# A transformer layer on one core: the later rows of the ada weight are asked for from GpSimd's queue instead of the sync engine's

## The chip, the cores and the metric

The kernel runs on one core of a Trainium2 chip. Its time is the device time of one execution in microseconds (us); of several executions the median is given. A core has a matrix engine (PE), a vector engine (DVE), an activation engine (ACT), GpSimd (POOL) and a sync engine (SP). Each runs its own instructions in order and waits on semaphores. Transfers between the chip's memory and the on-chip buffer are asked for by an instruction in some engine's queue, here SP's or POOL's, and are then moved by 16 DMA engines that all queues share.

## What is computed

One layer for 256 tokens of width 2048, in float32. A conditioning vector gives nine modulation vectors of 2048 each, and these shift, scale and gate three sub-layers:

```python
ada = (jax.nn.silu(c) @ w_ada + b_ada)[:, None, :]          # w_ada: 2048 x 18432
sh1, sc1, g1, sh2, sc2, g2, sh3, sc3, g3 = jnp.split(ada, N_ADA, axis=-1)
h = _swiglu(_modulate(x, sh1, sc1), ffn1_w_in, ffn1_w_out)
x = _layernorm(ALPHA * x + 0.5 * (1 + g1) * h, ln1_g, ln1_b)
h = _token_mixer(_modulate(x, sh2, sc2), w_in, ...)         # attention and mLSTM heads
x = _layernorm(ALPHA * x + (1 + g2) * h, ln2_g, ln2_b)
h = _swiglu(_modulate(x, sh3, sc3), ffn2_w_in, ffn2_w_out)
x = _layernorm(ALPHA * x + 0.5 * (1 + g3) * h, ln3_g, ln3_b)
```

All weights are read once from memory. The product with `w_ada` has one row on the left, so it needs 151 MB of weights and hardly any arithmetic.

## The kernel before

**The big products.** Each weight matrix comes in pieces of 1 MB, `raw` tiles, of which three buffers exist. `load_w` (L379) asks for a piece on SP (L383 or L387), ACT casts it to a rounded `hi` part (L155), DVE subtracts to get the remainder `lo` (L156), and PE multiplies hi by hi, hi by lo and lo by hi (L420 to L422, or L425 and L426). There are six `hi` and six `lo` buffers of half a piece each. A `raw` buffer is free for SP's next request when DVE's last subtraction of it has ended.

**The ada product** is spread over the whole run beneath the big products. It has 18 units of 16 rows; a row is 128 x 1024 numbers, 0.5 MB. For every row a DMA fills a tile `ar`, and DVE multiplies it by a column of silu(c) and adds it to an accumulator (`ada_acc`, L168 for the first row, L170 for the others). The accumulator is `acc`, or a part of the tile `gate`. When the 16 rows of a unit are in, its tail splits the accumulator into hi and lo (`alo`, L156), sums it over the partitions with PE (`bc`, L183) and stores columns (`pair_tail`) or a gate row (`gate_tail`). `gate_tail` also asks POOL for a piece of `b_ada` (L212), which may land only after the split has read the accumulator beneath it.

**Which rows are asked for where.** The first unit is loaded at the start on SP (`first_ada0`, L905). The next three units (`first_ada`, L937) have three `ar` buffers and are asked for from POOL, but for three rows. The remaining 14 units, 224 rows, go through the class `AdaQueue`: `pump(n)` is called after each weight piece with a rate (1 to 1.42 rows) and traces that many rows through `ada_rows` (L186 to L191), whose DMA at L189 has two `ar` buffers. These are the later rows. Row k + 2 can be asked for only when DVE has added row k.

**The order of the work.** The program is traced in Python, and a scheduler in the tile framework orders each engine's queue by its own estimates of when an instruction's inputs are ready; at the boundaries between the sub-layers the DVE order is written by hand. PE's order is that of the code. `pinned` (L141) and `issue_after` add ordering edges on DVE and ACT.

**POOL's other work:** a few memsets, the `pow` that gives reciprocal roots (L287: `rs`, `mr` at the three boundaries, `rr` in the mixer), the `b_ada` pieces at L212 and the layer-norm parameters `lg`, `lb` at L595 and L596.

**Stages by time:** the start and the first columns of FFN 1 to 226 us, the rest of its first product to about 520, its second product to 750, a boundary to about 790, the mixer to 1150, a boundary, FFN 2 from about 1180 to the end. The last row is asked for at 1518 us.

Of the kernel before, what the change touches and what calls it, by code (L numbers as in the profile page):

```python
# [14 lines left out]
P = 128  # L15
# [17 lines left out]
def layer_kernel(  # L33
# [8 lines left out]
    V, S, G_, PE, SP = nc.vector, nc.scalar, nc.gpsimd, nc.tensor, nc.sync  # L42
# [123 lines left out]
    def ada_acc(acc, raw, k):  # L166
        if k == 0:
            V.tensor_scalar_mul(acc, raw, csil[:, k:k + 1])  # L168
        else:
            V.scalar_tensor_tensor(out=acc, in0=raw, scalar=csil[:, k:k + 1], in1=acc,  # L170
                                   op0=ALU.mult, op1=ALU.add)
# [14 lines left out]
    def ada_rows(acc, src, tag):  # L186
        for k in range(KD):
            raw = ap.tile(list(acc.shape), F32, tag="araw", bufs=2, name=f"ar{tag}_{k}")
            SP.dma_start(raw, src[k * P:(k + 1) * P])  # L189
            ada_acc(acc, raw, k)  # L190
            yield  # L191

# [26 lines left out]
    class AdaQueue:  # L219
# [4 lines left out]
        def pair(self, v, j, where=None, stage=0):  # L224
            self.units.append((where, stage, lambda acc: ada_rows(acc, pair_cols(v, j), f"{v}_{j}"),
                               lambda acc: pair_tail(acc, v, j), [P, 2, 512], f"{v}_{j}"))

        def gate(self, v, s, *where, stage=0):
            for j in range(2):
                cols = w_ada[0, :, v * D + j * 1024:v * D + (j + 1) * 1024]  # L230
                self.units.append((where[j], stage, lambda acc, cols=cols, j=j: ada_rows(acc, cols, f"{v}_{j}"),
                                   lambda acc, j=j: gate_tail(acc, v, j, s), [P, 1024], f"{v}_{j}"))
# [1485 lines left out]
```

## Time and profile before

| | |
|---|---|
| median of 3 runs | 1874.08 us (1870.46 to 1882.13) |
| the profiled execution | 1878.46 us, span of its instructions 1876.8 us |
| PE busy | 1829.0 us, 97% of the span |
| DVE busy | 1465.0 us, 78% |
| ACT busy | 911.8 us, 49% |
| POOL busy | 62.2 us, 3% |
| moved by DMA | 510.74 MB, mean 272 GB/s |
| `ar` rows asked for from SP, from POOL | 230, 45 |

The times differ from run to run by some tenths of a per cent. A busy PE is not always PE at its peak, so what PE waits for is read from the list of waits. In a row of that list, or of a group of instructions, the name behind the arrow is that of the work that ended the wait. SP and POOL instructions that ask for a transfer appear under the line that asks, and the time to landing is counted from the start of the request to the semaphore of the transfer.

### The profile page before, as it was taken

The page shows a single profiled execution, that of the slowest core. Times are in us where ns is not written, and L with a number is a line of the kernel's source. Part 1 is how long each engine was busy: PE and PEld are TensorE (multiplying, and loading weights), DVE is VectorE, ACT ScalarE, POOL GpSimd, SP SyncE. Part 2 cuts the span into 40 slices and gives each one's busy share as a digit, 9 for nine tenths or more (in the row PEclk, how much of TensorE's full clock was granted, in tenths as well). Part 3 has the DMA queues.
Part 4 walks back from the last instruction along what each step waited for, and adds up shares of the span by engine and source line. Part 5 has one row for each costly group of instructions (what it writes and reads, how often), then busy time and mean ns, then how long its engine had stood idle before and what let it go on. Part 6 is the DMA issues. An engine that isn't in the chain of part 4 may idle for free.

```text
span 1876.8 us, 29775 instructions
## 1 busy us (share of the span) xinstructions
PE 1829.0 (97%) x11881; PEld 1673.8 (89%) x11881; DVE 1465.0 (78%) x1883; ACT 911.8 (49%) x1320; POOL 62.2 (3%) x92
## 2 busy tenths in 40 slices
PE   7999999999999999999989999999999999999997
PEld 5999999999998888699989887888999999988887
DVE  6888989778788886878879788988977766574655
ACT  3554363443454433845556545565444454554441
POOL 1211200000000000100000000000000000000000
PEclk9999999999999999999999999999999999999999
DMA  9988978999998898489978894998878776666664
GB/s 365 383 279 294 333 232 274 313 312 325 296 315 305 309 329 296 136 301 331 316 254 307 303 314 142 307 305 265 271 253 265 260 241 193 201 202 204 205 204 146
DMA packets 283906, 510.74 MB, mean 272 GB/s; under 512 B 10834, under 2 KB 134386, under 8 KB 282744
## 3 DMA queue, kind: packets, MB, share of 16 engines
q1 hardware_dynamic: 275656, 477.90, 75.0%
q0 software_dynamic: 8112, 30.95, 4.8%
q8 instruction: 93, 1.52, 0.3%
q14 instruction: 45, 0.37, 0.1%
HBM read 506.71 MB, written 2.10 MB: 271 GB/s over the span
## 4 chain that ended last, share of the span: by engine, by line
PE 38%; DMA 10%; DVE 8%; issue 2%; ACT 2%; POOL 0%; DVEq 0%; ACTq 0%; SPq 0%; POOLq 0%
PE gu_f L425 9%; DMA ar<-in_w_ada_dram 7%; PE gu_f L426 4%; PE o_f L421 4%; PE o_f L420 4%; PE o_f L422 4%; PE fs L425 3%; DMA raw_fh<-in_ffn_w_in_dram 2%; DVE acc L170 2%; PE fs L426 1%; DVE gate L170 1%; PE fh L425 1%; PE b_mv L421 1%; PE b_mv L420 1%; PE b_mv L422 1%
## 5 line engine op out<-in xcount | busy, mean ns | idle before, releaser
L170 DVE SCALAR_TENSOR_TENSOR acc<-ar,csil,acc 128x1024 f32<-128x1024 f32 (+1 forms) x167 | 211.7, 1269 | 74.3 <-DMA ar<-in_w_ada_dram 73.7
L425 PE MATMUL gu_f<-x_f,hi_f2i 128*128 128x512 f32 x768 | 251.8, 382 | 0.0
L422 PE MATMUL s<-x_f,lo_s 128*128 128x256 f32 x768 | 211.9, 276 | 0.8 <-DVE lo_s L156 0.7
L420 PE MATMUL s<-x_f,hi_s 128*128 128x256 f32 x768 | 212.2, 277 | 0.2 <-ACT x_f L336 0.2
L421 PE MATMUL s<-x_f,hi_s 128*128 128x256 f32 x768 | 212.0, 276 | 0.0
L426 PE MATMUL gu_f<-x_f,lo_f2i 128*128 128x256 f32 x768 | 209.3, 273 | 0.0
L422 PE MATMUL gu_f<-x_f,lo_f1i 128*128 128x256 f32 x640 | 176.4, 276 | 1.4 <-DVE lo_f1i L156 1.3
L421 PE MATMUL gu_f<-x_f,hi_f1i 128*128 128x256 f32 x640 | 176.0, 275 | 0.0
L420 PE MATMUL gu_f<-x_f,hi_f1i 128*128 128x256 f32 x640 | 176.0, 275 | 0.0
L156 DVE TENSOR_TENSOR lo_f2o<-raw_f2o,hi_f2o 128x1024 fp32r<-128x1024 f32 x86 | 105.2, 1225 | 86.9 <-ACT hi_f2o L155 86.8
L156 DVE TENSOR_TENSOR lo_f2i<-raw_f2i,hi_f2i 128x1024 fp32r<-128x1024 f32 x96 | 117.5, 1224 | 65.7 <-ACT hi_f2i L155 64.8
L425 PEld LDWEIGHTS gu_f<-x_f,hi_f2i 128*128 128x128 f32 x768 | 145.1, 189 | 20.3
L155 ACT CAST hi_s<-raw_s 128x1024 fp32r<-128x1024 f32 x96 | 99.5, 1051 | 128.7 <-PE s L421 77.0
L422 PEld LDWEIGHTS s<-x_f,lo_s 128*128 128x128 f32 x768 | 147.9, 193 | 1.2 <-DVE lo_s L156 1.2
L421 PEld LDWEIGHTS s<-x_f,hi_s 128*128 128x128 f32 x768 | 147.9, 193 | 0.4 <-DVE x_f L339 0.4
L420 PEld LDWEIGHTS s<-x_f,hi_s 128*128 128x128 f32 x768 | 147.8, 193 | 0.3 <-ACT x_f L336 0.3
L426 PEld LDWEIGHTS gu_f<-x_f,lo_f2i 128*128 128x128 f32 x768 | 147.4, 192 | 0.2
L155 ACT CAST hi_f2o<-raw_f2o 128x1024 fp32r<-128x1024 f32 x86 | 90.0, 1047 | 115.7 <-PE o_f L422 107.5
L155 ACT CAST hi_f2i<-raw_f2i 128x1024 fp32r<-128x1024 f32 x96 | 100.4, 1045 | 91.3 <-PE gu_f L425 65.3
L155 ACT CAST hi_f1o<-raw_f1o 128x1024 fp32r<-128x1024 f32 x86 | 88.5, 1047 | 113.7 <-DMA raw_f1o<-in_ffn_w_out_dram 55.0
L170 DVE SCALAR_TENSOR_TENSOR gate<-ar,csil,gate 128x1024 f32<-128x1024 f32 (+1 forms) x94 | 117.6, 1252 | 29.0 <-DMA ar<-in_w_ada_dram 28.9
L155 ACT CAST hi_f1i<-raw_f1i 128x1024 fp32r<-128x1024 f32 x80 | 81.3, 1049 | 111.6 <-DMA raw_f1i<-in_ffn_w_in_dram 80.2
(449 smaller groups left out, 5095.4 us busy)
## 6 DMA issues: line engine op xcount, KB each, us to landing
ar<-in_w_ada_dram SPq DMA_DIRECT2D x230, 512.0 KB, 5.5
raw_f2i<-in_ffn_w_in_dram SPq DMA_DIRECT2D x48, 1024.0 KB, 5.2
raw_s<-in_ffn_w_in_dram SPq DMA_DIRECT2D x47, 1024.0 KB, 7.6
raw_f1o<-in_ffn_w_out_dram SPq DMA_DIRECT2D x44, 1024.0 KB, 7.3
raw_f2o<-in_ffn_w_out_dram SPq DMA_DIRECT2D x44, 1024.0 KB, 5.2
raw_f1i<-in_ffn_w_in_dram SPq DMA_DIRECT2D x40, 1024.0 KB, 7.8
ar<-in_w_ada_dram POOLq DMA_DIRECT2D x45, 512.0 KB, 6.4
raw_mxo<-in_w_out_dram SPq DMA_DIRECT2D x16, 1024.0 KB, 7.7
```

The source lines that it names most:

```text
L155: S.copy(hi, src)
L156: return V.tensor_tensor(out=lo, in0=src, in1=hi.bitcast(F32), op=ALU.subtract)
L170: V.scalar_tensor_tensor(out=acc, in0=raw, scalar=csil[:, k:k + 1], in1=acc, op0=ALU.mult, op1=ALU.add)
L420: PE.matmul(o, ah, bh, start=start, stop=False)
L421: PE.matmul(o, ah, bl, start=False, stop=False)
L422: PE.matmul(o, al, bh, start=False, stop=stop)
L425: PE.matmul(o, ah, x.rearrange("p s (a n) -> p s n a", a=2), start=start, stop=False)
L426: PE.matmul(o[:, T:], al, woven(x[:, 0]), start=False, stop=stop)
```

## The change

One word in `ada_rows`: the DMA of the 224 later rows is traced on GpSimd instead of the sync engine.

```diff
     def ada_rows(acc, src, tag):
         for k in range(KD):
             raw = ap.tile(list(acc.shape), F32, tag="araw", bufs=2, name=f"ar{tag}_{k}")
-            SP.dma_start(raw, src[k * P:(k + 1) * P])
+            G_.dma_start(raw, src[k * P:(k + 1) * P])
             ada_acc(acc, raw, k)
             yield
```

Since the scheduler estimates other arrival times for the rows, it also places some instructions of DVE and ACT differently. PE's order is unchanged.

SP's queue in the mixer (about 910 to 940 us), the difference from before to after: `raw_fb` are weight pieces of the attention heads' queries, `ar_0_2` to `ar_0_5` rows of the unit that makes the first half of gate 2.

```order
 L383 DMA raw_fb_9975<-in_w_in_dram 128x4x512
 L383 DMA raw_fb_10054<-in_w_in_dram 128x4x512
-L189 DMA ar_0_2_9962<-in_w_ada_dram 128x1024
-L189 DMA ar_0_3_10043<-in_w_ada_dram 128x1024
 L383 DMA raw_fb_10126<-in_w_in_dram 128x4x512
-L189 DMA ar_0_4_10112<-in_w_ada_dram 128x1024
-L189 DMA ar_0_5_10115<-in_w_ada_dram 128x1024
 L383 DMA raw_fb_10218<-in_w_in_dram 128x4x512
```

The rows no longer stand between the weight pieces.

DVE's queue at the same place: L156 makes the `lo` parts of those weight pieces, L170 adds the rows to their accumulator.

```order
 L156 TENSOR_TENSOR lo_fb_9978<-raw_fb_9975,hi_fb_9977 128x1024
+L170 SCALAR_TENSOR_TENSOR acc_0_9893<-ar_0_2_9962,csil,acc_0_9893 128x1024
 L156 TENSOR_TENSOR lo_fb_10006<-raw_fb_9975,hi_fb_10005 128x1024
-L170 SCALAR_TENSOR_TENSOR acc_0_9893<-ar_0_2_9962,csil,acc_0_9893 128x1024
+L170 SCALAR_TENSOR_TENSOR acc_0_9893<-ar_0_3_10043,csil,acc_0_9893 128x1024
 L156 TENSOR_TENSOR lo_fb_10057<-raw_fb_10054,hi_fb_10056 128x1024
-L170 SCALAR_TENSOR_TENSOR acc_0_9893<-ar_0_3_10043,csil,acc_0_9893 128x1024
 L156 TENSOR_TENSOR lo_fb_10085<-raw_fb_10054,hi_fb_10084 128x1024
+L170 SCALAR_TENSOR_TENSOR acc_0_9893<-ar_0_4_10112,csil,acc_0_9893 128x1024
+L170 SCALAR_TENSOR_TENSOR acc_0_9893<-ar_0_5_10115,csil,acc_0_9893 128x1024
 L156 TENSOR_TENSOR lo_fb_10129<-raw_fb_10126,hi_fb_10128 128x1024
```

Each of these rows is added one `lo` earlier than before; the same happens at many places of the first 1250 us.

POOL's queue about 1000 us, where it has other work: `rr` is the `pow` for the mLSTM heads' normalization, the rows are those of the second half of gate 2.

```order
+L189 DMA ar_1_3_11004<-in_w_ada_dram 128x1024
+L189 DMA ar_1_4_11080<-in_w_ada_dram 128x1024
 L287 TENSOR_TENSOR rr<-ss,mhalf 128x8
-L212 DMA gate<-in_b_ada_dram 128x512 x2
+L189 DMA ar_1_5_11155<-in_w_ada_dram 128x1024
+L189 DMA ar_1_6_11158<-in_w_ada_dram 128x1024
```

The `pow` now stands behind row 4 of its unit and ahead of row 5, and the two `b_ada` pieces that followed it come later among the rows.

## The prediction

> **What bounds the kernel now.** I read the page first, then the list of who waits for whom, for PE, for SP's queue and, stage by stage, for DVE; then the timeline of single rows.
>
> ```profile
> span 1876.8 us, 29775 instructions
> PE 1829.0 (97%) x11881; PEld 1673.8 (89%) x11881; DVE 1465.0 (78%) x1883; ACT 911.8 (49%) x1320; POOL 62.2 (3%) x92
> ...
> ar<-in_w_ada_dram SPq DMA_DIRECT2D x230, 512.0 KB, 5.5
> ...
> ar<-in_w_ada_dram POOLq DMA_DIRECT2D x45, 512.0 KB, 6.4
> ```
>
> PE is busy for 97% of the span, so nothing that happens to the rows can be worth more than what PE waits for while the moved rows run. That is the list of PE's waits between 226 and 1518 us, the time from the first moved request to the last:
>
> ```profile
> PE sps L1428 <- DVE dm L1434: 5.0, 1, 5.0
> PE o_mx L422 <- DVE ylo L156: 2.9, 1, 2.9
> PE fh L425 <- DVE hT L1642: 2.8, 1, 2.8
> ...
> PE bc L183 <- DVE alo L156: 2.0, 2, 1.6
> PE pr_fb L422 <- DVE lo_fb L156: 1.5, 1, 1.5
> PE gu_f L422 <- DVE lo_f1i L156: 1.3, 2, 1.1
> ...
> PE b_fv L421 <- DVE lo_fv L156: 1.0, 1, 1.0
> PE b_mv L421 <- DVE lo_mv L156: 0.8, 1, 0.8
> ```
>
> Each ends with DVE (columns: total us, times, longest). Together they are 5.0 + 2.9 + 2.8 + 2.0 + 1.5 + 1.3 + 1.0 + 0.8 = 17.3 us, 0.9% of the time. This is the ceiling of a gain. For a loss there is no such ceiling: DVE works in order, and where it stands at a row that has not landed, the `lo` parts that PE needs stand behind it. DVE's waits by stage (330 to 480, 480 to 750, 790 to 950, 950 to 1130, 1180 to 1320 us), in that order:
>
> ```profile
> DVE acc L170 <- DMA ar<-in_w_ada_dram: 14.5, 7, 3.9
> DVE lo_f1i L156 <- ACT hi_f1i L155: 10.8, 5, 4.0
> DVE gate L170 <- DMA ar<-in_w_ada_dram: 10.7, 6, 4.9
> DVE acc L168 <- DMA ar<-in_w_ada_dram: 3.1, 1, 3.1
> ...
> DVE acc L170 <- DMA ar<-in_w_ada_dram: 21.0, 18, 2.5
> DVE lo_f1o L156 <- ACT hi_f1o L155: 10.9, 11, 3.0
> DVE o_f L538 <- PE o_f L422: 5.7, 1, 5.7
> ...
> DVE acc L170 <- DMA ar<-in_w_ada_dram: 13.9, 11, 3.0
> DVE gate L170 <- DMA ar<-in_w_ada_dram: 2.1, 3, 1.1
> DVE lo_mv L156 <- ACT hi_mv L155: 1.6, 2, 1.2
> DVE gate L168 <- DMA ar<-in_w_ada_dram: 1.4, 1, 1.4
> ...
> DVE acc L170 <- DMA ar<-in_w_ada_dram: 15.5, 9, 4.7
> DVE gate L170 <- DMA ar<-in_w_ada_dram: 9.1, 6, 3.7
> DVE dm L1433 <- ACT dm L1432: 4.3, 2, 2.6
> DVE acc L168 <- DMA ar<-in_w_ada_dram: 2.0, 1, 2.0
> ...
> DVE gate L170 <- DMA ar<-in_w_ada_dram: 3.5, 3, 2.9
> ```
>
> So DVE waits for rows 14, 18, 15, 16 and 3 times in these stages. In the first two it also waits 10.8 and 10.9 us for ACT's casts, so there it has room; in the mixer (790 to 1130) the rows are nearly all that it waits for, and it has little.
>
> **The change part by part.** *The request.* Does a row on SP stand behind the weight pieces? Here are a DVE addition and SP's next row, and a DVE addition and POOL's next row in the stage whose rows POOL asks for already:
>
> ```profile
> 842.95 1.29 DVE L170 SCALAR_TENSOR_TENSOR acc<-ar,csil,acc 128x1024 f32<-128x1024 f32 x1
> ...
> 844.27 0.37 SPq L189 DMA_DIRECT2D ar<-in_w_ada_dram  x1
> ...
> 117.50 1.28 DVE L170 SCALAR_TENSOR_TENSOR gate<-ar,csil,gate 128x1024 f32<-128x1024 f32 x1
> ...
> 119.09 0.72 POOL L937 DMA_DIRECT2D ar<-in_w_ada_dram  x1 [2.87 <-DVE gate L170]
> ```
>
> SP asks 0.03 us after the addition that frees the buffer (842.95 + 1.29 = 844.24), so it stands at the row before the buffer is free: the row is not late, what waits is the weight piece behind it. POOL asks 0.31 us after (117.50 + 1.28 = 118.78). The moved row is therefore asked for 0.28 us later, not sooner.
>
> *The landing.* The page's medians are 6.4 us from POOL and 5.5 from SP, 0.9 more. But the median of all rows flatters SP for those rows that DVE waits for: they are slow ones, behind weight pieces in the same queue. On the chain of waits:
>
> ```profile
> 935.93 5.10 SPq L383 DMA_DIRECT2D raw_fbk<-in_w_in_dram  x2
> 943.43 0.34 SPq L189 DMA_DIRECT2D ar<-in_w_ada_dram  x1
> ...
> 943.43 8.65 DMA ar<-in_w_ada_dram
> ```
>
> A row asked for behind two pieces took 8.65 us. In a queue of its own it would not stand behind them, so the excess of the rows that matter lies between nothing and 0.9 us. I take half, 0.45, since rows of both kinds are waited for. With the 0.28 us a round trip gets 0.73 us longer; the ends are 0.28 and 1.18. An end below zero is a rival of its own.
>
> The Trainium skill, "DMA: Bandwidth & Descriptors", section "Latency and other measured facts", speaks against the change: it gives about 1 us to the first byte for a transfer from GpSimd and about 0.6 us for one from the sync engine. By it the landing would cost an estimated 0.4 us more, the round trip 0.68 us, and the sum below would hardly differ; the trace's medians agree in sign and are further apart (0.9 us).
>
> *What DVE pays.* With two buffers, the time for which DVE stands at one row is time that the next one, already on its way, gains; so one row of two pays: waits x 0.73 / 2. By stage: 14 gives 5.1 us, 18 gives 6.6, 15 gives 5.5, 16 gives 5.8, 3 gives 1.1; 24.1 us of DVE in all.
>
> *What PE pays.* 330 to 480: DVE's room (10.8 us) covers 5.1, but PE stood at `lo_f1i` for 1.3 us already, so the lead is short at times: 1 us (0 to 5.1). 480 to 750: none of the PE waits above is from this stage, and 10.9 + 5.7 us of room cover 6.6: 0. 790 to 950: room is 1.6 us in the rows above; PE already feels `lo_fv`, `lo_mv` and `lo_fb`, 3.3 us of 17.4 that DVE waits for rows there. Between that share (1.0) and all that is left (3.9) I take 3. 950 to 1130: room 4.3 us, but PE's waits of 5.0 and 2.9 lie here: 3 (0 to 5.8). 1180 to 1320: 1 us. Sum +8.
>
> *The weight pieces on SP* lose what stood ahead of them.
>
> ```profile
> SPq L189 <- DVE acc L170: 190.8, 120, 4.2
> ...
> SPq L189 <- DVE gate L170: 112.2, 63, 5.3
> ...
> L155 ACT CAST hi_fh<-raw_fh 128x1024 fp32r<-128x1024 f32 x32 | 32.9, 1050 | 29.8 <-DMA raw_fh<-in_ffn_w_in_dram 26.8 <-PE fh L426 1.8 <-PE fh L425 1.2
> ```
>
> SP stood at rows for 190.8 + 112.2 = 303 us. That costs nothing where the `raw` buffers are full anyway. At `raw_fh`, after the second boundary, it does: ACT waits 26.8 us for these pieces and PE 2.8 us at `fh`. Earlier requests give back at most those 2.8 us and what else is lost to raw pieces, unseen; I take -3.
>
> *DVE's order.* Rows stand one `lo` earlier, so a `lo` can come one addition (1.28 us) later. At the four places where PE already stands at a `lo` (`pr_fb`, `gu_f`, `b_fv`, `b_mv`) that is 0 to 5.1 us; I take 1.
>
> *POOL.* 224 requests of 0.72 us are 161 us of an engine that is 3% busy. Ahead of them in the queue stand the L212 requests, which wait for `alo`; in DVE's order `alo` precedes the addition that frees the next row's buffer, so nothing is held. Behind a row stand the `pow` instructions: a request just begun can delay `rr` by up to 0.31 + 0.72 = 1.0 us; at the boundaries no row is due. `lg` waits long for PE, with no row behind it that is due. I take 0.
>
> Sum: 8 - 3 + 1 = +6 us. The profiled execution took 1878.46 us, 1.7 more than its span and 4.4 more than the median of the three runs; +6 makes 1884.5 for it, and 1880 as a median.
>
> **The rivals.** *Rows arrive sooner.* In a queue of their own they share the DMA engines with the weight pieces instead of following them. Then DVE's row waits shrink, and PE gets back some or all of 17.3 us: 1857 to 1869, the middle 1863. For it: the 8.65 us row. Against it: POOL's rows run beside SP's weight pieces in the stage before 226 us, and their median is 6.4.
>
> The Trainium skill, "DMA: Bandwidth & Descriptors", section "Queues, rings and completion order", has the rule that would do this: each DMA engine takes turns between queues that have work. No run here shows it by itself.
>
> *Nothing to measure.* The lead of the `lo` parts covers everything: 1874, from 1870 to 1876. For it: 480 to 750, where 21.0 us of row waits reach PE nowhere.
>
> *DVE becomes the bound in the mixer*, the rival on the other side. If its lead over PE is used up, every longer round trip passes through: at 1.18 us, 14, 15, 16 and 3 waits give 48 x 1.18 / 2 = 28 us, so 1902; at half that, 1888. It decides once DVE's added 5.5 us in 790 to 950 exceeds its room there. For it: PE waits for `lo` parts already; against it: DVE's lead is restored at the boundaries.
>
> **How the numbers follow.** Forecast (1876 to 1888): 0.45; nothing: 0.22; sooner: 0.13; the mixer bound: 0.20. Likeliest is 1880. The range, 1862 to 1900, leaves out the last part of each tail and takes in the run-to-run spread of some 4 us. About 1% (1855 to 1893) is what a measurement of this kernel can tell from no change: faster takes more than the whole ceiling, 0.05; slower is most of the mixer rival, 0.17; within it 0.78.
>
> **What would show it.** The rows under L189 on POOL, asked for 0.3 us after DVE's addition, landing at 6 to 6.4 us; DVE's waits for rows up from 17.4 and 26.6 us in the mixer; PE's waits at `lo_fv`, `lo_mv`, `lo_fb` longer, at `fh` shorter. Rows landing under 5.5 us would make the forecast wrong towards faster, PE waits of 10 us or more at mixer `lo` parts towards slower, and so would a POOL wait that holds a row.

## The result: 2.5% slower, outside the range

The changed kernel takes 1923.03 us (median of 4, 1916.45 to 1928.78), the kernel before, run beside it, 1874.03 us. The ratio is 1.0254, with a 95% interval from 1.0206 to 1.0303: 49 us lost, where the prediction had 6 and a range up to 1900. The profiled execution after took 1920.51 us. Medians leave out two far slower executions, one of 2365.48 us in run e4 and one of 4934.1 us of the kernel before beside it.

From the page of the kernel after: span, busy time, and the rows of two kinds of transfers (number, size, median us from request to landing).

```profile
span 1918.8 us, 29789 instructions
...
PE 1842.2 (96%) x11881; PEld 1680.0 (88%) x11881; DVE 1465.9 (76%) x1883; ACT 912.6 (48%) x1320; POOL 205.0 (11%) x316
...
ar<-in_w_ada_dram POOLq DMA_DIRECT2D x269, 512.0 KB, 5.4
...
raw_f1o<-in_ffn_w_out_dram SPq DMA_DIRECT2D x44, 1024.0 KB, 7.4
```

DVE's busy time is what it was (1465.0 before). PE's own busy time grew by 13.2 us with the same 11881 instructions, so 29 of the 42 us that the span grew are waits of PE, and 13 are PE being slower. The median landing of a row, 5.4 us, is no worse than SP's 5.5 before. By the signs named in the prediction a landing under 5.5 us would have meant a faster kernel, so that sign misled: one median over the whole run does not show the later landing by stage that the table below has. The other sign came true, PE waits of 10 us or more at mixer `lo` parts: `lo_m`, `lo_fb` and `lo_fv` make 10.9 us in the list below.

Where it was lost, by the first matmul of each stage: the start and the first product of FFN 1 end at the same time (526.6 us before, 526.8 after); the second product with its boundary, to the first `mo` matmul (the first product of the mixer), takes 256.1 us instead of 233.0; the mixer with its boundary, to the first `ge` (the first of FFN 2), 419.0 instead of 400.0. FFN 2 gives nothing. So 23 us went in the second product, where the prediction had 0, and 19 in the mixer.

PE's waits after, 226 to 1518 us:

```profile
PE bc L183 <- ACT ahi L155: 7.4, 1, 7.4
PE o_f L421 <- DVE lo_f1o L156: 6.0, 4, 2.3
PE pr_m L422 <- DVE lo_m L156: 4.5, 3, 2.7
PE ptp L1308 <- DVE s L1293: 4.2, 1, 4.2
PE pr_fb L422 <- DVE lo_fb L156: 3.4, 2, 2.4
PE gu_f L422 <- DVE lo_f1i L156: 3.1, 1, 3.1
PE b_fv L421 <- DVE lo_fv L156: 3.0, 2, 2.3
```

New are the waits for `lo_f1o`, and one of 7.4 us for `ahi`, the hi part of the accumulator, at the end of the second product, where before PE waited for nothing. ACT's timeline shows what held `ahi` (start, length, instruction, idle time before it): it stands behind casts of the last weight pieces, and these waited 8.18 and 0.70 us for the pieces to land.

```profile
753.74 1.99 ACT L155 CAST hi_f1o<-raw_f1o 128x1024 fp32r<-128x1024 f32 x2 [8.18 <-DMA raw_f1o<-in_ffn_w_out_dram]
756.43 1.99 ACT L155 CAST hi_f1o<-raw_f1o 128x1024 fp32r<-128x1024 f32 x2 [0.70 <-DMA raw_f1o<-in_ffn_w_out_dram]
758.33 0.61 ACT L155 CAST ahi<-acc 128x512 fp32r<-128x512 f32 x1
```

Behind both stands DVE, whose subtractions free the buffers of the pieces. Its row waits in the five stretches of the prediction, in that order (the same clock times, so after 750 us slightly earlier work):

```profile
DVE acc L170 <- DMA ar<-in_w_ada_dram: 16.3, 8, 4.0
DVE gate L170 <- DMA ar<-in_w_ada_dram: 13.1, 8, 3.6
...
DVE acc L170 <- DMA ar<-in_w_ada_dram: 41.1, 24, 3.8
...
DVE lo_f1o L156 <- ACT hi_f1o L155: 6.0, 6, 3.0
...
DVE acc L170 <- DMA ar<-in_w_ada_dram: 16.2, 10, 3.6
DVE gate L170 <- DMA ar<-in_w_ada_dram: 13.0, 8, 3.0
...
DVE gate L168 <- DMA ar<-in_w_ada_dram: 1.8, 1, 1.8
...
DVE acc L170 <- DMA ar<-in_w_ada_dram: 13.4, 6, 5.4
DVE gate L170 <- DMA ar<-in_w_ada_dram: 11.1, 7, 4.1
...
DVE gate L170 <- DMA ar<-in_w_ada_dram: 8.4, 5, 3.5
```

From 480 to 750 us they doubled, from 21.0 to 41.1 us, and from 790 to 950 they went from 17.4 to 31.0. Summed over the additions of all 224 later rows, DVE now stands 155.0 us, against 100.6 before.

How this gets through to PE is seen in what ACT waits for from 480 to 750 us; first after, then before:

```profile
ACT hi_f1o L155 <- DMA raw_f1o<-in_ffn_w_out_dram: 66.8, 20, 7.8
ACT hi_f1o L155 <- PE o_f L422: 27.4, 17, 3.4
```

```profile
ACT hi_f1o L155 <- DMA raw_f1o<-in_ffn_w_out_dram: 55.0, 21, 5.0
ACT hi_f1o L155 <- PE o_f L422: 45.2, 29, 3.5
```

Where ACT waits for PE, the casts are ahead and PE sets the pace. That fell from 45.2 to 27.4 us, and the waits for a weight piece grew from 55.0 to 66.8 us: a piece can be asked for only after DVE's last subtraction of an older one.

### The profile page after: what moved, and what is told of

Its sections match the earlier page's. It is cut to its first block, busy times and chain, and to the rows that moved or that the text cites. A ratio compares the mean times of both kernels' runs of the same rounds, so it can differ in the third digit from the quotient of the medians.

```text
span 1918.8 us, 29789 instructions
## 1 busy us (share of the span) xinstructions
PE 1842.2 (96%) x11881; PEld 1680.0 (88%) x11881; DVE 1465.9 (76%) x1883; ACT 912.6 (48%) x1320; POOL 205.0 (11%) x316
## 4 chain that ended last, share of the span: by engine, by line
PE 36%; DMA 10%; DVE 7%; issue 4%; ACT 2%; POOL 1%; DVEq 0%; POOLq 0%; ACTq 0%; SPq 0%
DMA ar<-in_w_ada_dram 9%; PE gu_f L425 9%; PE gu_f L426 4%; PE o_f L420 4%; PE o_f L421 4%; PE o_f L422 4%; PE fs L425 3%; PE fs L426 1%; PE fh L425 1%; PE o_mx L420 1%; DVE gate L170 1%; PE o_mx L421 1%; PE o_mx L422 1%; DMA raw_fh<-in_ffn_w_in_dram 1%; DVE acc L170 1%
## 5 line engine op out<-in xcount | busy, mean ns | idle before, releaser
L170 DVE SCALAR_TENSOR_TENSOR acc<-ar,csil,acc 128x1024 f32<-128x1024 f32 (+1 forms) x167 | 211.6, 1268 | 107.3 <-DMA ar<-in_w_ada_dram 106.9
L189 POOL DMA_DIRECT2D ar<-in_w_ada_dram x224 | 143.4, 640 | 999.3 <-DVE acc L170 437.5
L156 DVE TENSOR_TENSOR lo_f2o<-raw_f2o,hi_f2o 128x1024 fp32r<-128x1024 f32 x86 | 105.2, 1224 | 86.8 <-ACT hi_f2o L155 86.7
L156 DVE TENSOR_TENSOR lo_f2i<-raw_f2i,hi_f2i 128x1024 fp32r<-128x1024 f32 x96 | 117.4, 1223 | 65.6 <-ACT hi_f2i L155 64.8
L425 PEld LDWEIGHTS gu_f<-x_f,hi_f2i 128*128 128x128 f32 x768 | 145.1, 189 | 20.4
L170 DVE SCALAR_TENSOR_TENSOR gate<-ar,csil,gate 128x1024 f32<-128x1024 f32 (+1 forms) x94 | 117.5, 1251 | 48.0 <-DMA ar<-in_w_ada_dram 47.9
```

The source lines that it names most:

```text
L156: return V.tensor_tensor(out=lo, in0=src, in1=hi.bitcast(F32), op=ALU.subtract)
L189: G_.dma_start(raw, src[k * P:(k + 1) * P])
L425: PE.matmul(o, ah, x.rearrange("p s (a n) -> p s n a", a=2), start=start, stop=False)
```

## The experiments

The change does two things at once: it moves the requests to another queue, and, through the scheduler's estimates, it moves instructions on DVE and ACT. To part them, kernels were built in which the order on named engines is held to a written list, by ordering edges alone; engines that are not named keep the scheduler's order. e11 below, held in this way on DVE, ACT and SP, takes as long as the kernel before (1.0002), so the holding itself costs nothing that shows.

All numbers in one place. *Asked* is the mean time from the end of the DVE work that frees a buffer to the request of the next transfer into it, *landed* from the request to the last of the 16 closing packets of that transfer in the DMA records (the semaphore reports it some 0.45 us later); both for the second product. Their sum is the trip of a buffer, from free to full. In e4 the 4-byte transfers look like closing packets, so its landings cannot be told apart. "DVE at rows" is its row wait from 480 to 750 us. Stages, waits and trips are read from one profiled execution of each kernel; four of those that take as long as before or less (before, e4, e6, e11) agree within 0.3 us for the second product and differ by up to 7.5 us for the mixer.

| kernel | ratio to before (95%) | second product, mixer, us | DVE at rows, us | rows: asked + landed, us | pieces: asked + landed, us |
|---|---|---|---|---|---|
| before | 1 | 233.0, 400.0 | 21.0 | 0.07 + 5.22 | 0.42 + 6.55 |
| after | 1.0254 (1.0206 to 1.0303) | 256.1, 419.0 | 41.1 | 0.34 + 5.42 | 0.03 + 6.97 |
| e1, rows on POOL, old order | 1.0163 (1.0138 to 1.0188) | 248.6, 414.3 | 37.3 | 0.34 + 5.52 | 0.03 + 7.06 |
| e2, rows on SP, new order | 1.0186 (1.0159 to 1.0214) | 253.0, 409.1 | 38.2 | 0.03 + 5.33 | 0.30 + 6.56 |
| e3, e1 and pieces held back | 1.0256 (1.0230 to 1.0283) | 256.3, 419.5 | 44.1 | 0.34 + 5.56 | 0.62 + 6.89 |
| e4, SP, a small transfer ahead of each row | 1.0018 (0.9994 to 1.0042) | 232.7, 396.5 | 23.0 | 0.36 + (not separable) | (not separable) |
| e5, SP, DVE longer | 1.0076 (1.0056 to 1.0096) | 240.9, 404.8 | 21.0 | 0.03 + 5.30 | 0.39 + 6.66 |
| e6, SP, half rows | 0.9960 (0.9942 to 0.9979) | 233.0, 393.8 | 12.2 | 0.15 + 4.46 | 0.29 + 5.76 |
| e7, POOL, half rows | 1.0201 (1.0174 to 1.0228) | 250.6, 404.5 | 41.3 | 0.40 + 4.86 | 0.03 + 6.78 |
| e8, one POOL queue | 1.0161 (1.0109 to 1.0212) | 248.3, 407.8 | 30.8 | 0.40 + 5.33 | 0.67 + 6.93 |
| e9, pieces on POOL, rows on SP | 1.0227 (1.0172 to 1.0282) | 248.6, 415.4 | 39.8 | 0.03 + 5.74 | 0.32 + 7.34 |
| e10, SP, rows one later | 1.0158 (1.0114 to 1.0203) | 258.7, 400.1 | 42.2 | 0.07 + 5.42 | 0.12 + 6.39 |
| e11, SP, rows asked later | 1.0002 (0.9977 to 1.0027) | 233.0, 401.3 | 20.4 | 0.28 + 4.98 | 0.45 + 6.35 |
| e12, SP, rows and pieces asked later | 1.0032 (1.0006 to 1.0059) | 239.5, 399.1 | 25.6 | 0.29 + 5.17 | 0.62 + 6.60 |

### The queue, or the order?

e1 is the changed kernel with DVE's and ACT's instructions in the order of before; e2 is the kernel before with them in the order of after. PE's order is the same in all.

```diff
+    for eng, text in held_order.items():
...
+        for p, q in zip(names, names[1:]):
+            tc.add_manual_dep(traced[q], p, mybir.DependencyInfo(mybir.DependencyClass.NoSync,
+                                                                 mybir.DependencyReason.DATA), reason="held order")
```

> Rows are asked for from GpSimd's queue as in the changed kernel, but VectorE and ScalarE go through their instructions in the order of the kernel before (ordering alone, no wait between engines is added). Theory ORDER (the new order puts row additions ahead of the low parts that TensorE needs, the queue itself is nearly harmless): 1874 to 1888 us, the first boundary at 750 to 758 us. Theory QUEUE (a request on GpSimd's queue makes each row later: 0.3 us more between the buffer's release and the request, 0.72 us per request instruction): 1915 to 1930 us, as the changed kernel, first boundary at about 773 us, and VectorE's idle time before row additions near 155 us as now. Theory SHARING (weight pieces, no longer held behind rows on the sync engine, take their place in the DMA engines at the wrong times): also 1910 to 1930 us.

> The mirror image: rows are asked for from the sync engine as in the kernel before, but VectorE and ScalarE go in the changed kernel's order. ORDER: 1910 to 1930 us, with TensorE waiting for low parts (lo_f1o, lo_m, lo_fb) and for the first boundary's ahi as in the changed kernel. QUEUE and SHARING: 1870 to 1882 us, the kernel before.

e1 took 1904.19 us, e2 1907.74: neither theory alone. The queue by itself costs 1.6%, the order by itself 1.9%, and together they cost 2.5%, less than their sum. In both, DVE stands longer at rows from 480 to 750 us; e1 and then e2:

```profile
DVE acc L170 <- DMA ar<-in_w_ada_dram: 37.3, 24, 3.4
```

```profile
DVE acc L170 <- DMA ar<-in_w_ada_dram: 38.2, 19, 4.5
```

In e2 the transfers are nearly as quick as before (5.36 us for a row from free buffer to landing, before 5.29). There DVE only comes to the row sooner, one `lo` earlier, and what it would have done first now stands behind the wait. In e1 DVE's order is that of before, and the row is later by 0.57 us. The wait of PE for `ahi` is there in both, 8.8 and 7.8 us.

e3 holds 144 requests for pieces on SP in e1 back until the addition that freed the row ahead of them in the old queue.

```diff
+    for pair in held_back.split():
+        w, r = (f"I-{k}" for k in pair.split(":"))
...
+        tc.add_manual_dep(traced[w], r, mybir.DependencyInfo(mybir.DependencyClass.Sync,
+                                                             mybir.DependencyReason.DATA), reason="held back")
```

> Rows on GpSimd's queue, the old order on VectorE and ScalarE, and 144 requests for weight pieces on the sync engine each wait for the VectorE addition that frees the buffer of the row that stood ahead of them in the kernel before, so that the pieces are asked for as late as they were there. SHARING: 1874 to 1888 us while the first of these three kernels stays above 1905. ORDER: the same as the first of the three within 6 us. QUEUE: 1915 to 1930 us in both.

It took 1920.56 us, 16 more than e1. So the loss does not come from pieces being asked for too early, as SHARING had it; with the rows on POOL, asking for pieces early is a gain, as the prediction's step on SP had it.

### Is it the later request?

In e4 SP asks, ahead of every row, for a transfer of 4 bytes that waits for the same addition. e11 has no further transfer: the row waits for a GpSimd memset of one column, which waits for the addition. In e12 the weight pieces wait so too. All three keep the order of before on DVE, ACT and SP.

```diff
+            first = SP.dma_start(late[0:1, n % 16:n % 16 + 1], w_ada[0, 0:1, n:n + 1]).ins
```

```diff
-            SP.dma_start(raw, src[k * P:(k + 1) * P])
+            first = relay(freed[0])
+            asked = SP.dma_start(raw, src[k * P:(k + 1) * P]).ins
+            tc.add_manual_dep(asked, first.name, mybir.DependencyInfo(mybir.DependencyClass.Sync,
+                                                             mybir.DependencyReason.DATA), reason="late")
```

> The kernel before, rows on the sync engine, VectorE, ScalarE and the sync engine held in the order of before; ahead of each of the 224 rows the sync engine asks for a transfer of 4 bytes that waits for the same VectorE addition, so that each row is asked for about 0.3 us later, the delay that GpSimd's queue has. Theory REQUEST (the later request is what the queue costs): 1893 to 1910 us, VectorE's idle time ahead of row additions at 125 to 140 us instead of 101. Rival LANDING (rows and weight pieces in two queues share the DMA engines, and that makes the rows late): at most 1884 us.

> The kernel before, all requests on the sync engine and in its order, VectorE and ScalarE in the order of before; only each of the 224 row requests waits for a tiny GpSimd memset that itself waits for the VectorE addition, so that the row is asked for some tenths of a microsecond later with no further transfer in the queue. Theory REQUEST (the later request costs, and in the run with the 4-byte transfers it was hidden by these): 1885 to 1905 us, the second product of FFN 1 at 240 to 250 us where the kernel before takes 233. Rival (a later request is taken up by the queue ahead of it, as in that run): 1870 to 1882 us, the second product at 232 to 236 us.

> The same, and the weight pieces' requests wait for such a memset too: both kinds asked for later, one queue, the sync engine's. If the later requests are why the single GpSimd queue lost 15 us in the second product although its transfers landed as soon after the request as in the kernel before: 1893 to 1912 us, the second product at 243 to 253 us. If the delay of requests is not it: 1870 to 1884 us, and what the single GpSimd queue lost stays open.

e4 took 1876.58 us, e11 1872.76: no difference from before (1.0018 and 1.0002), as LANDING and the rival of e11 expected. In the timeline of e11, a row's request stands 0.25 us behind the addition that ends at 608.08 us (start, length, engine, instruction):

```profile
606.80 1.28 DVE L170 SCALAR_TENSOR_TENSOR acc<-ar,csil,acc 128x1024 f32<-128x1024 f32 x1 [0.56 <-DMA ar<-in_w_ada_dram]
...
608.20 0.10 POOL L191 MEMSET late<- 128x1 f32 x1 [4.01 <-DVE acc L170]
608.33 0.37 SPq L202 DMA_DIRECT2D ar<-in_w_ada_dram  x1
```

On SP the delay vanishes in the queue: asked 0.21 us later, the rows land 0.24 us sooner after the request (0.28 + 4.98 against 0.07 + 5.22). So REQUEST falls for SP's queue. With the pieces late as well (e12, 1880.29 us) the second product takes 239.5 us, 6.5 more, while the whole is 0.3% slower, as expected for the case that the delay is not what the single POOL queue, the next experiment, loses.

### One queue or two?

e8 asks for rows and for pieces from POOL, e9 for the pieces from POOL and for the rows from SP; DVE and ACT in the order of before. The pieces of the first columns stay on SP. In the second product e8's one queue asks for rows and pieces in the same sequence as SP before.

```diff
+        queue = SP if name[0] == "s" and name[1].isdigit() else G_
         raw = wp.tile([P, nk, w], F32, tag="raw", bufs=3, name=f"raw_{name}")
...
-            SP.dma_start(raw, src)
+            queue.dma_start(raw, src)
```

> Rows and weight pieces (from the end of the first columns on) are all asked for from GpSimd's queue, so that they stand behind one another again as in the kernel before, only in GpSimd's queue; VectorE and ScalarE in the order of before. Theory TURNS (what makes rows and pieces land later is that two queues with work share the DMA engines, so that the first of two transfers no longer ends early): the span to the first boundary and through the mixer as in the kernel before within 8 us each, 1872 to 1892 us in all, the excess at the boundaries where GpSimd's own work stands among the requests. Rival START (a transfer from GpSimd's queue takes longer to begin, by whatever queue it shares): 1900 to 1930 us, first boundary at 762 us or later as in the run with rows on GpSimd in the old order.

> Swapped: weight pieces from GpSimd's queue, rows from the sync engine's; VectorE and ScalarE in the order of before. TURNS: two queues again, so rows land later than in the kernel before although they are asked for from the sync engine: 1893 to 1925 us. START: the rows, which VectorE waits for, are quick, only the pieces are late: 1874 to 1892 us.

e9 took 1912.65 us, e8 1903.05. The pages' rows for the moved kind and its neighbour, e8 and then e9:

```profile
ar<-in_w_ada_dram POOLq DMA_DIRECT2D x269, 512.0 KB, 5.6
...
raw_f1o<-in_ffn_w_out_dram POOLq DMA_DIRECT2D x44, 1024.0 KB, 7.6
```

```profile
ar<-in_w_ada_dram SPq DMA_DIRECT2D x230, 512.0 KB, 5.8
...
raw_f1o<-in_ffn_w_out_dram POOLq DMA_DIRECT2D x44, 1024.0 KB, 7.8
```

e9 came out as TURNS expected, e8 as START did (its first boundary is at 775.1 us, too), so neither theory holds both. The landings tell more than the times.

e9 shows that a second queue makes a row late: SP asks for it 0.03 us after its buffer is free, DVE's order is that of before, and it lands in 5.74 us instead of 5.22. The pieces now come through another queue and no longer take their place between the rows; that they come too early is not the reason, since in e3, where they are held back, the rows still need 5.56. From 330 to 1150 us a row lands 5.0 to 5.3 us after its request in all six kernels that have one queue and whole rows and whose closing packets can be told apart (before, e2, e5, e10, e11, e12, on SP), 5.2 us in e8, and 5.4 to 5.6 us in the four with two (after, e1, e3, e9); a piece 6.3 to 6.5 on SP and 6.7 in e8, against 6.9 to 7.2 with two queues. So START falls as a reason for late rows: in one POOL queue they land nearly as they do in one SP queue.

But e8 did not win the time back: 248.3 us for the second product, as much as e1 and e9 lose with two queues. On POOL's queue a request that comes later is not made good. Its pieces are asked for 0.25 us later than before and land 0.38 us later still, its rows 0.33 and 0.11. e12, with later requests on SP, shows 6.5 of these 15 us; why the landing does not shorten on POOL's queue as it does on SP's stays open. So two things lengthen the trips, a second queue and requests from POOL, and e1 has both.

### Does DVE have room?

e5 puts one short DVE instruction behind each later row addition (0.28 us each by its row in the trace; DVE's busy time grows by 40.2 us, 0.18 us each).

```diff
             ada_acc(acc, raw, k)
+            row = [i for i in nc.cur_bb.bb.instructions][-1]
+            extra.append((V.tensor_reduce(out=idle_v[:, 0:1], in_=triu1[:, :128], axis=AX.X, op=ALU.add).ins, row))
```

> The kernel before in its own order, with one more short VectorE instruction (a sum over 128 numbers, about 0.2 us, its result unused) behind each of the 224 later row additions: about 16 us more VectorE work from 330 to 790 us, 16 us in the mixer, 9 us after it. Theory LOOP (VectorE has no room in the second product and in the mixer: what it waits for there, a cast, hangs on a piece whose buffer VectorE itself freed, so its lost time reaches TensorE nearly one for one): 1892 to 1910 us, with 8 to 16 us lost before the first boundary. Rival ROOM, as in the prediction (waits for ScalarE and the lead of the low parts cover such a loss): 1872 to 1884 us, and at most 4 us lost before the first boundary.

It took 1888.32 us, 15 us more by the medians, between the two expectations of LOOP and ROOM. In the second product, with its 40 rows, DVE got 40 x 0.18 = 7.2 us more work, stood at rows as long as before (21.0 us), and the product took 7.9 us longer: there DVE's time is PE's time. In the mixer 80 rows bring 14 us of work and PE pays 4.8; there is some room, though the mixer's time varies by a few us between like kernels.

e10 moves 158 of the row additions the other way, behind the `lo` that followed them.

> The kernel before, rows on the sync engine, with 158 of the 224 row additions one low part later in VectorE's order (a row and the low part behind it change places), the opposite of what the change's order did. Theory ORDER (rows early in VectorE's queue hold the low parts up): VectorE's idle time ahead of row additions falls from 101 to 60 to 90 us, and the time to 1860 to 1874 us. Rival (any order but the one of before loses, because the lead of the low parts and the buffers are matched to it): 1885 us or more.

It took 1901.67 us, as the rival expected, which refutes that rows are simply better late. The mixer is unchanged (400.1 us), the second product 26 us longer, and DVE stands 42.2 us at rows there. An addition that comes later also frees its buffer later, which is the likely reason but was not shown apart: SP's order was free here, and in that stretch some rows came to stand behind one more weight piece. Together with e2 it shows that moving many rows in DVE's order costs some 30 us either way.

### Halves

e6 and e7 ask for each row in two halves of 128 x 512, and add them one by one, in the same two buffers, so that four halves are on their way. The order is the scheduler's.

```diff
+            for h in range(2):
+                part = (slice(None), h) if len(acc.shape) == 3 else (slice(None), slice(h * 512, (h + 1) * 512))
+                raw = row_halves[len(asked) % 4]
+                asked.append(raw)
+                SP.dma_start(raw, src[k * P:(k + 1) * P][part])
+                ada_acc(acc[part], raw, k)
```

> The kernel before with each row asked for and added in two halves of 128 x 512 in the same buffers, four halves in flight where there were two rows. A half can be asked for as soon as the addition that frees its own half has ended. If the round trip of rows over two buffers is what VectorE loses: its idle time ahead of row additions falls from 101 us to 30 to 70, and the time to 1858 to 1870 us (the ceiling is the 17.3 us of TensorE's waits). If the additional 224 VectorE instructions (fixed costs) outweigh that: 1875 to 1895 us.

> The same halves, asked for from GpSimd's queue as in the changed kernel: 448 requests of some 0.7 us. If the row round trip is what the change made longer and VectorE pays for it: 1875 to 1895 us, most of the loss gone. If the loss is not in the row's round trip: 1915 to 1930 us, as the changed kernel.

On SP this is the shortest time of the study, as expected for the case that the round trip is what DVE loses: 1867.58 us, ratio 0.9960 (0.9942 to 0.9979), a gain of 0.4%. DVE's row wait from 480 to 750 us, in e6:

```profile
DVE acc L170 <- DMA arhalves<-in_w_ada_dram: 12.2, 10, 2.2
```

On POOL it took 1912.68 us, between its two expectations: the wait is 41.3 us again. The scheduler orders DVE's work anew in both, so e6 does not tell the halves from the order, nor e7 the queue from the order. Three whole row buffers were not tried.

## Why the prediction was wrong, step by step

**The request** was read rightly. In the timeline of after:

```profile
842.95 1.28 DVE L170 SCALAR_TENSOR_TENSOR acc<-ar,csil,acc 128x1024 f32<-128x1024 f32 x1 [2.07 <-DMA ar<-in_w_ada_dram]
...
844.54 0.72 POOL L189 DMA_DIRECT2D ar<-in_w_ada_dram  x1 [3.23 <-DVE acc L170]
```

POOL asks 0.31 us after the addition. That this delay costs time was a step without proof: e4 and e11 show that as late a request on SP costs nothing, while e8 shows no such recovery on POOL's queue.

**The landing.** I took 0.45 us of the 0.9 between two medians. Worked out for all transfers of the second product, the row lands 0.20 us later in after and 0.30 in e1; the whole trip grew by 0.47 and 0.57 us, where I had 0.73. So the size of this term was not what failed, and in after the landing is the smaller part of it (with the same order on DVE, e2, a row lands in 5.33 us, in after in 5.42). Its reason was off: the 8.65 us row behind two pieces let me think that a queue of its own would relieve a row, and e9 shows that it makes rows later. The sum left out the pieces, which land 0.4 to 0.5 us later in two queues (6.55 to 6.97, and 7.06 in e1); but as SP asks for them 0.39 us sooner, their trip hardly grew (6.97 to 7.00 us, and 7.09 in e1). By the rule of the Trainium skill, "DMA: Bandwidth & Descriptors", section "Queues, rings and completion order", each DMA engine takes turns between queues with work. The landings agree with it, though the rule does not say who gains: in e9 both kinds came later.

**What DVE pays** is a step that failed. Waits x 0.73 / 2 charged only the 18 rows that DVE already waited for from 480 to 750 us, 6.6 us; measured were 20.1 more, and 16.3 in e1, where the order is that of before. A row that just came in time before is late now, and the number of waits grew as well (18 to 24 there). An estimate made after the runs fits better: with N transfers through n buffers, and no room, each pays 1/n of what its trip grows. For e1, which has the queue's effect without the order's: 40 rows / 2 x (5.86 - 5.29) + 43 pieces / 3 x (7.09 - 6.97) = 11.4 + 1.7 = 13.1 us, and measured were 15.6 for the product. The same estimate gives 7.0 for e12 (measured 6.5), 17.8 for e8 (15.3), 19.5 for e9 (15.6), 19.9 for e3 (23.3) and -3.0 for e11 (0), so it is right to some 4 us where DVE's order is that of before. For e2 it gives nothing and 20.0 were lost, so it does not price an order.

**What PE pays** is the step that failed most: "480 to 750: none of the PE waits above is from this stage, and 10.9 + 5.7 us of room cover 6.6: 0". It was 23 us; the queue alone makes 15.6 of it in e1, the order alone 20.0 in e2. (The first product, priced at 1 us, lost 0.2.) DVE's waits for ACT's casts are no room, since the cast waits for a piece whose buffer DVE frees: a late DVE makes the cast late, too. PE's list of waits was empty there because the `lo` parts came just in time; e5 shows that the next 7 us of DVE come through whole. The mixer was priced at 6 and lost 19, 14.3 by the queue alone and 9.1 by the order alone. The list of PE's waits, 17.3 us, also left out rows of 6.1 us, so the ceiling of a gain was 23.4; the miss does not hang on that.

**A cost that the sum did not have**: after a wait, PE is slower for a while. Around the 7.4 us wait of after (window, its length, PE busy, granted clock, DMA share, GB/s):

```profile
740.00:750.00 10.00, 8.71 (x40) 1.00 0.56 209
750.00:760.00 10.00, 2.55 (x10) 0.82 0.98 353
760.00:770.00 10.00, 10.00 (x40) 0.84 0.49 179
770.00:780.00 10.00, 10.00 (x48) 1.00 0.01 2
```

PE was busy for all of 760 to 770 us, and its clock was 0.84. In the records of the clock it is halved from 756.4 to 763.2 us, and 3.2 us at half rate in ten make 0.84. Over the run the mean granted clock went from 0.996 to 0.991, which is 1842 x 0.005 = 9 of the 13.2 us by which PE's busy time grew; the rest stays open. The Trainium skill, "TensorE: Matmul & The Clock Gate", section "Part 1: The HAM clock gate (the "warmup" mystery)", has a rule for it: after an idle window of about 3.4 us the clock is halved until the array has been busy about as long. The trace agrees in the length, since the clock is halved here for 3.4 us at a time or twice that, but not in the idle time: shorter waits of PE were followed by it, too, as one of 3.0 us by half the clock from 654.0 to 657.4 us, and four more of 2.3 to 3.1 us between 310 and 990 us.

**The weight pieces on SP.** The 2.8 us wait at `fh` went to 0.2, as forecast, and in e3 holding the pieces back cost 16 us more.

**DVE's order** is the other step that failed. Priced at 1 us from 0 to 5.1, it costs 35 us by itself (e2, 1907.74 against 1872.28). I charged it only where PE already stood at a `lo`. Its price shows at the rows, where DVE stands 38.2 us instead of 21.0 in e2: it comes sooner to a row that comes no sooner. e10 loses as much by the opposite move, so the order of before was matched to its transfers; why it is so narrow was not shown.

**POOL** at nothing was right: no wait for a `pow` is longer than 0.7 us. Five rows were asked for 1.5 to 2.3 us after their buffer was free, too few to matter.

**The rivals.** "Rows arrive sooner" is refuted by e1 and e9, where they land later. "DVE becomes the bound in the mixer" was the right mechanism in too small a place: the stage without PE waits was the one with no room, and it added the larger share. "Nothing to measure" took that stage for a proof of cover.

**What stays open**: why queue and order, 32 and 35 us alone, make 49 together; which of the moved instructions cost most; and why POOL's single queue in e8 loses as much as two queues.

## What to carry to other kernels

Where two streams fill few buffers and the compute engine is 97% busy, an empty list of waits does not mean room: multiply the longer trip by the number of transfers over the number of buffers, and take as cover only a wait that the delayed engine does not itself cause. Here two streams that feed the same work did best in one queue, and that queue had to be SP's: the same two streams in POOL's queue lost 1.6%. After moving a request look at what the scheduler did with the consumers' order, since it can cost as much as the queue. Rows in halves in the same buffers gave the only gain here, 0.4%.

## What was not expected of the hardware

- A request that comes 0.2 to 0.3 us later on SP's queue was made up for in the landing (rows 5.22 to 4.98 us in e11), and the time did not change.
- Two queues made both kinds of transfers land later than one: rows 5.22 to 5.74 us, on SP's queue in both cases (e9), pieces 6.55 to 7.06 us, on SP's queue in both (e1), though there they were asked for 0.39 us sooner.
- One queue of POOL's for both kinds cost as much as two queues: 1.6% in e8 and in e1.
- The clock was halved in steps of 3.4 us, also after PE waits of only 2.3 to 3.1 us.
